# Windowed attention: the sink as a column of each head's scores, and sums transposed before they are inverted

## The chip, the cores and the metric

The kernel runs on one core of a Trainium2 chip. The metric is the device time of one execution in microseconds (us); lower is better. The core's engines run their own queues of instructions, in the order in which the program lists them: PE (matrix multiplies and transposes; PEld is its weight load), DVE (vector), ACT (scalar, here the exponentials and copies), POOL (general), SP (which issues most of the transfers). An instruction that waits for a semaphore holds everything behind it on its own engine.

## The reference

One layer of a diffusion transformer on 1024 latent tokens with 256 context tokens, width 1024: two attention parts side by side, merged by gates, then a SwiGLU feed-forward part with a convolution. The change lies in the first attention part: 8 heads in 2 groups of 4 that share keys and values, each block of 128 queries against its neighbouring blocks and the context, with one learned sink logit per head that takes part in the softmax but has no value.

```python
def _sink_softmax(scores, sink):
    sink = sink.astype(jnp.float32)[:, :, None, None]
    m = jnp.maximum(jnp.max(scores, axis=-1, keepdims=True), sink)
    e = jnp.exp(scores - m)
    return e / (jnp.sum(e, axis=-1, keepdims=True) + jnp.exp(sink - m))
...
        band = ((jnp.abs(q_pos[:, None] - k_pos[None, :]) <= WINDOW)
                & (k_pos[None, :] >= 0) & (k_pos[None, :] < n_tok))
        mask = jnp.concatenate([band, ctx_mask], axis=1)
        scores = jnp.where(mask, _gqa_scores(q_blk, k_blk), -jnp.inf)
        return _gqa_values(_sink_softmax(scores, sink), v_blk)
```

The second attention part is global: every query against all 1024 latent and 256 context keys, without a sink.

## The kernel before

Matrix operands are split into a high and a low part, so that most products are two or three multiplies. Attention fills the stretch from about 333 to 756 us of the span. It is made of 32 **units**: 16 of the windowed part (`br` 0), then 16 of the global part (`br` 1). A unit is one block `i` of 128 queries and one group `g` of four heads; names in the profile carry `br_i_g` and the head or key block behind it. In the windowed part a head has 256 latent columns for the first and last block, 384 for the others, and 256 context columns: 512 or 640 columns of scores.

What a unit does, with the lines of the profile:

- `lat(h)`, four times: PE multiplies queries and keys into the score tile `s` (two such tiles exist). DVE (L497) writes the negated scores to a tile `p` and keeps their running minimum with the negated sink, which gives `nm`, the negated maximum. ACT (L464) overwrites `p` with exp(score - maximum) and accumulates the row sum into `sm`. In the global part the context columns of all four heads are reduced beforehand (`cxp`, L515, tile `p_x`) and have an exponential and a sum `smc` of their own.
- `norm` (L518 to L525): in the windowed part DVE adds the sink to `nm` (L522, `f`), ACT takes the exponential of that (L523), DVE adds it to the sums (L524) and inverts the four columns of sums (L525). In the global part DVE adds `smc` to `sm` and inverts.
- `rows` (L527 to L538): PE transposes the 128x4 inverted sums to 4x128 (`str`, L529), ACT copies them into the tile `rb` (L532), and three transfers on SP's queue spread them over the partitions of `rb`, by way of DRAM. Two `rb` tiles exist.
- `value_steps`: for each key block PE transposes `p` of the four heads (`ptr`, L562), ACT makes the high part (`pth`, L571) and DVE the low part (`ptl`, L572), or POOL both for a few blocks; PE multiplies both with the values into `av` (L583, L584). At the end (`out_step`) ACT copies `av` out, POOL moves its upper half down, DVE adds the halves in the windowed part (`ot`, L595; in the global part POOL does), and POOL multiplies by `rb` and splits the result for the next product.

The value steps of a unit run among the scores of the next. The order on each engine is fixed when the program is built, by a scheduler that places the instructions by their data and buffers; the loop over `units` only gives it the steps. Tiles `p` come from a ring of eight in the pool `att`, used in turn by all units of both parts, so a new unit's first tiles lie on those of the unit two before it. Beside attention POOL and the transfers prepare weights for the next stage (`lwb`), which needs neither PE nor DVE here.

## Time and profile before

| | |
|---|---|
| median of 3 runs | 1546.9 us (1546.41 to 1548.97) |
| the profiled execution, its own time | 1549.18 us |
| its span, first to last instruction | 1547.4 us |
| granted clock of PE, mean | 0.998 |
| windowed units | from 336 to about 470 us of the span |
| global units | from about 462 to 756 us |
| one windowed unit in the steady part | 8.36 us (its sums' transpose at 399.44, the next unit's at 407.80) |

The profile counts times from the start of the span. A row of the timeline gives start, length, engine, line, operation and tiles of one instruction (or of several alike), and in brackets how long the engine had stood idle before it and whose result ended that. A row of the windows gives for a stretch the busy time and the instructions of PE, PEld, DVE, ACT and POOL, then the clock, the share of the transfer engines and GB/s. A row of a tile's view gives the shortest, the median and the longest length of its instructions in ns.

### The profile page before, as it was taken

How to read it: one execution, taken by the hardware profiler on the slowest of the kernel's cores; microseconds unless marked ns; L12 is line 12 of the kernel's file. 1: busy time of each engine (PE TensorE's matmuls, PEld its weight loads, DVE VectorE, ACT ScalarE, POOL GpSimd, SP SyncE). 2: the span in 40 equal slices, each digit the busy share in tenths (PEclk: the TensorE clock that was granted, in tenths of full speed). 3: DMA queues.
4: the chain of work that ended last, by engine and by line, in shares of the span. 5: the costliest groups of instructions: out<-in, count | busy, mean ns of one | idle time of the engine just before them, and what ended most of it. 6: DMA issues, size and time to landing. Idle time of an engine off the chain costs nothing.

```text
span 1547.4 us, 21962 instructions
## 1 busy us (share of the span) xinstructions
PE 1524.8 (99%) x7652; PEld 1269.2 (82%) x7652; DVE 1172.8 (76%) x1783; ACT 801.9 (52%) x1420; POOL 751.8 (49%) x697
## 2 busy tenths in 40 slices
PE   9999999999999999999999999999999999999997
PEld 7888888878887788888788988888888888888886
DVE  7588847638888667788575879898888887657797
ACT  5422223448888666698422674544444444435543
POOL 0375303426667466565423555766676675021063
PEclk9999999999999999999999999999999999999999
DMA  9667663322237565533452223233334446996723
GB/s 379 236 224 252 232 236 93 113 80 70 64 88 179 113 144 130 116 87 83 157 142 76 83 82 123 89 116 109 109 109 112 114 115 170 360 287 213 257 87 109
DMA packets 111873, 229.73 MB, mean 148 GB/s; under 512 B 13489, under 2 KB 27313, under 8 KB 111666
## 3 DMA queue, kind: packets, MB, share of 16 engines
q1 hardware_dynamic: 96464, 199.20, 38.5%
q0 software_dynamic: 10400, 20.19, 8.4%
q10 hardware_dynamic: 4898, 8.94, 1.6%
q8 instruction: 60, 0.98, 0.3%
q14 instruction: 51, 0.42, 0.1%
HBM read 177.09 MB, written 65.87 MB: 157 GB/s over the span
## 4 chain that ended last, share of the span: by engine, by line
PE 92%; DVE 4%; ACT 2%; issue 1%; POOL 1%; DMA 0%; DVEq 0%; ACTq 0%; POOLq 0%
PE ptr L562 6%; PE g L96 4%; PE g L95 4%; PE g L94 4%; PE p L94 4%; PE p L96 4%; PE p L95 4%; PE b L94 3%; PE b L96 3%; PE b L95 3%; PE av L583 3%; PE av L584 3%; PE s L451 3%; PE s L452 2%; PE c L95 2%; PE d L95 2%
## 5 line engine op out<-in xcount | busy, mean ns | idle before, releaser
L572 DVE TENSOR_TENSOR ptl<-ptr,pth 128x512 fp32r<-128x512 f32 x188 | 123.4, 684 | 32.6 <-ACT pth L571 31.8
L91 DVE TENSOR_TENSOR ld<-rd,hd 128x1024 fp32r<-128x1024 f32 x77 | 97.5, 1285 | 48.6 <-ACT hd L86 45.0
L562 PE MATMUL ptr<-ident,p 128*128 128x128 f32 x816 | 127.0, 277 | 5.8 <-DVE ptl L572 2.7
L571 ACT CAST pth<-ptr 128x512 fp32r<-128x512 f32 x188 | 105.6, 586 | 50.2 <-PE ptr L562 35.3
L464 ACT ACTIVATE p<-p,nm 128x1024 f32<-128x1024 f32 (+2 forms) x128 | 125.1, 979 | 10.5 <-DVE p L497 9.9
L86 ACT CAST hd<-rd 128x1024 fp32r<-128x1024 f32 x77 | 79.5, 1050 | 84.6 <-PE p L96 50.8
L562 PEld LDWEIGHTS ptr<-ident,p 128*128 128x128 f32 x816 | 95.1, 140 | 33.7 <-DVE ptl L572 7.7
L583 PE MATMUL av<-pth,VT 128*128 128x512 f32 x236 | 105.0, 445 | 1.2 <-ACT pth L571 0.9
L94 PE MATMUL p<-hd 128*128 128x512 f32 x264 | 103.2, 391 | 0.0
L96 PE MATMUL p<-hd,ld 128*128 128x512 f32 x264 | 102.7, 389 | 0.0
L95 PE MATMUL p<-ld,hd 128*128 128x512 f32 x264 | 102.7, 389 | 0.0
L96 PE MATMUL g<-hh,wlg 128*128 128x512 f32 x256 | 99.7, 390 | 0.4 <-POOL wlg L91 0.4
L94 PE MATMUL g<-hh,whg 128*128 128x512 f32 x256 | 99.9, 390 | 0.0
L95 PE MATMUL g<-hl,whg 128*128 128x512 f32 x256 | 99.6, 389 | 0.0
L584 PE MATMUL av<-ptl,VT 128*128 128x512 f32 x236 | 97.5, 413 | 0.5 <-POOL ptl L91 0.5
L91 POOL TENSOR_TENSOR wlg<-wg,whg 128x512 fp32r<-128x512 f32 x32 | 45.2, 1420 | 99.6 <-ACT whg L86 85.2
L497 DVE TENSOR_SCALAR_CACHE_REDUCE p<-s,cvt,nmc 128x1024 f32<-128x1024 f32 x64 | 84.5, 1338 | 7.4 <-PE ptr L562 5.5
L451 PE MATMUL s<-KL,q 128*128 128x512 f32 (+2 forms) x192 | 77.0, 401 | 0.8 <-DVE p_x L515 0.6
L88 POOL TENSOR_SCALAR pth<-prw 128x512 fp32r<-128x512 f32 x48 | 30.9, 644 | 93.1 <-PE av L583 43.8
L86 ACT CAST wS<-s 128x512 fp32r<-128x512 f32 x76 | 45.3, 621 | 52.0 <-POOL s L1166 51.2
L452 PE MATMUL s<-KL,q 128*128 128x512 f32 (+2 forms) x192 | 71.5, 372 | 0.0
L86 ACT CAST wA<-ru 128x512 fp32r<-128x512 f32 x57 | 35.5, 623 | 60.5 <-PE d L96 32.4
(403 smaller groups left out, 4922.5 us busy)
## 6 DMA issues: line engine op xcount, KB each, us to landing
wml<-in_wmodT_dram SPq DMA_DIRECT2D x48, 512.0 KB
ru<-in_w_up_dram SPq DMA_DIRECT2D x38, 512.0 KB
rd<-td SPq DMA_DIRECT2D x55, 256.0 KB
...
```

Source lines behind the costliest of these rows:

```text
L86: cast[:] = [nc.scalar.copy(hi, src).ins]
L91: low[:] = [lo_eng.tensor_tensor(out=lo, in0=src, in1=hi.bitcast(F32), op=ALU.subtract).ins]
L94: nc.tensor.matmul(ps, a[0], b[0], start=start, stop=False, skip_group_check=resumed)
L95: nc.tensor.matmul(ps, a[0], b[1], start=False, stop=False, skip_group_check=resumed)
L96: return nc.tensor.matmul(ps, a[1], b[0], start=False, stop=stop, skip_group_check=resumed).ins
L451: nc.tensor.matmul(o, self.q[0][:, hs], ks, start=True, stop=False)
L464: nc.scalar.activation(p, s, AF.Exp, bias=nm[:, h:h + 1], scale=scale, accum_out=sm[:, h:h + 1])
L562: nc.tensor.transpose(tr[:, h * P:(h + 1) * P], self.pslice(h, n), ident)
L571: nc.scalar.copy(hi, tr)
L572: nc.vector.tensor_tensor(out=lo, in0=tr, in1=hi.bitcast(F32), op=ALU.subtract)
L583: nc.tensor.matmul(self.av, v, hi, start=first, stop=False)
L584: nc.tensor.matmul(self.av, v, lo, start=False, stop=self.left == 0)
```

## The change

The sink becomes a column. Eight fixed tiles `pa0` to `pa7` of 128x1024 take the place of the ring in the windowed part, one for each head (`g*4+h`). At the start DVE copies each head's negated sink once into column 641 of its tile (L830, eight copies of 128x1). A head's negated scores now end at column 640, right before it, and start at column `pad`+1. The exponential reads scores and sink together and writes them one column further left, so the sink's column is read, never overwritten, and serves all eight units of that head; its exponential lands in column 640, is in the accumulated sum, and is not read by the transposes. The instructions of L522, L523 and L524 of the windowed part are gone.

Sums are transposed first. PE transposes `sm` itself, and the reciprocal, now 4x128 on DVE from the transposed tile into `rb` (L531), takes the place of ACT's copy, in all 32 units. The reciprocal 128x4 of L525 is gone; of `norm` only the addition of `smc` in the global part is left.

The tiles `p` move from `att` to a pool of their own, `pp`, on the other side of the memory. After unit 15 it is released and allocated again as a ring of eight for the global part. In the built program `pa0` to `pa7` lie in ascending places; in the new ring `p1_0_0_x` lies on `pa0`, and `p1_0_0_0` to `p1_0_0_3` lie on `pa7`, `pa6`, `pa5`, `pa4`, the tiles of unit 15 (`0_7_1`). Before, `p1_0_0_0` to `p1_0_0_2` lay on tiles of unit 14 and only `p1_0_0_3` on one of unit 15.

Line numbers of the changed kernel are a few higher or lower: L497 became L500, L464 L466, L515 L520, L529 L528, L562 L561, L571 and L572 L570 and L571, L583 and L584 L582 and L583, L595 L594, L1047 L1055.

```diff
@@ -47,6 +47,7 @@
 GORD = 3, 4, 4, 1, 4
 PWB = 5
 DAH = 3
+SINK = 640
 D3AT = (7, 5), (7, 9), (4, 1), (4, 4), (4, 7), (4, 10), (5, 2)
 NXS = 5
 RAWB = 3
@@ -455,13 +456,14 @@
             self.nm = small(f"nm_{self.id}", (P, 4))
             self.sm = small(f"sm_{self.id}", (P, 4))
             self.other = negsink[:, self.g * 4:self.g * 4 + 4]
+            self.pad = 0 if self.br else SINK - NC - self.w
 
         def qscale(self, t):
             return t[:, self.i, self.g * 4:self.g * 4 + 4]
 
-        def soft(self, s, p, h, nm, sm, scale):
+        def soft(self, s, p, h, sm):
             with tc.issue_after(first_exp):
-                nc.scalar.activation(p, s, AF.Exp, bias=nm[:, h:h + 1], scale=scale, accum_out=sm[:, h:h + 1])
+                nc.scalar.activation(p, s, AF.Exp, bias=self.nm[:, h:h + 1], scale=-1.0, accum_out=sm[:, h:h + 1])
 
         def lat(self, h):
             kh = self.br * 2 + self.g
@@ -493,13 +495,16 @@
                 self.qk(s[:, 512:512 + NC], h, KC[0][:, kh])
                 o = s[:, 512 - w:512 + NC]
             hs = slice(h, h + 1)
-            p = p_tile(f"p{self.id}_{h}")[:, 0:T if self.br else self.w + NC]
-            nc.vector.tensor_scalar(out=p, in0=o, scalar1=self.qscale(nqs)[:, hs] if self.br else -1.0,
+            p = p_tile(f"p{self.id}_{h}") if self.br else pa[self.g * 4 + h]
+            sc = p if self.br else p[:, self.pad + 1:SINK + 1]
+            nc.vector.tensor_scalar(out=sc, in0=o, scalar1=self.qscale(nqs)[:, hs] if self.br else -1.0,
                                     scalar2=self.other[:, hs], op0=ALU.mult, op1=ALU.min, accum_out=self.nm[:, hs])
-            self.soft(p, p, h, self.nm, self.sm, -1.0)
-            self.pc[h, 0] = p
             if self.br:
-                self.soft(self.pc[h, 1], self.pc[h, 1], h, self.nm, self.smc, -1.0)
+                self.soft(p, p, h, self.sm)
+                self.soft(self.pc[h, 1], self.pc[h, 1], h, self.smc)
+            else:
+                self.soft(p[:, self.pad + 1:SINK + 2], p[:, self.pad:SINK + 1], h, self.sm)
+            self.pc[h, 0] = p[:, self.pad:]
 
         def cxp(self):
             kh = self.br * 2 + self.g
@@ -516,20 +521,14 @@
                                         op0=ALU.mult, op1=ALU.min, accum_out=self.other[:, h:h + 1])
 
         def norm(self):
-            hc = slice(self.g * 4, self.g * 4 + 4)
-            more = self.smc if self.br else small(f"f_{self.id}", (P, 4))
-            if not self.br:
-                nc.vector.tensor_tensor(out=more, in0=self.nm, in1=sinkb[:, hc], op=ALU.add)
-                nc.scalar.activation(more, more, AF.Exp)
-            nc.vector.tensor_tensor(out=self.sm, in0=self.sm, in1=more, op=ALU.add)
-            nc.vector.reciprocal(self.sm, self.sm)
+            nc.vector.tensor_tensor(out=self.sm, in0=self.sm, in1=self.smc, op=ALU.add)
 
         def rows(self):
             tr = pt_tile(f"str{self.id}")
             nc.tensor.transpose(tr[0:4, 0:P], self.sm, ident)
             self.rb = att.tile([P, 2, P], F32, tag="rb", name=f"rb{self.id}", bufs=2)
             row = self.rb[0:4, 0]
-            nc.scalar.copy(row, tr[0:4, 0:P])
+            nc.vector.reciprocal(row, tr[0:4, 0:P])
             dn = dpool.tile([4, P], F32, tag=f"dn{self.id}", name=f"dn{self.id}")
             tokens.append(f"dn{self.id}")
             nc.sync.dma_start(dn, row)
@@ -539,7 +538,7 @@
 
         def score_steps(self):
             steps = [lambda h=h: self.lat(h) for h in range(4)]
-            return steps + [self.norm]
+            return steps + [self.norm] * self.br
 
         def context(self):
             self.begin()
@@ -825,8 +824,13 @@
     def s_tile(name):
         return ps2.tile([P, T], F32, tag="s", name=name, bufs=2)
 
+    pp = tc.alloc_tile_pool(name="pp", bufs=1, side="right", reuse_waits="tile")
+    pa = [pp.tile([P, T], F32, tag=f"pa{n}", name=f"pa{n}") for n in range(8)]
+    for n in range(8):
+        nc.vector.tensor_copy(pa[n][:, SINK + 1:SINK + 2], negsink[:, n:n + 1])
+
     def p_tile(name):
-        return att.tile([P, T], F32, tag="p", name=name, bufs=8)
+        return pp.tile([P, T], F32, tag="p", name=name, bufs=8)
 
     def small(name, shape):
         return att.tile(list(shape), F32, tag=name.split("_")[0], name=name,
@@ -898,6 +902,9 @@
             ss = units[u].score_steps()
             if u + 2 < nu:
                 ss.append(units[u + 2].qprep)
+        if u == 16:
+            pp.release()
+            pp = tc.alloc_tile_pool(name="pp", bufs=1, side="right", reuse_waits="tile")
         if u == 29:
             first = branch_steps(1, w_b, (0, 1), att, (nc.gpsimd, nc.gpsimd), (0,),
                                  lambda: [ht(f"{a}wb1_0", (P, 8, P), R32) for a in "hl"])
@@ -932,6 +939,7 @@
     hput(*[f"VT{t}" for t in range(5)])
     first[2]()
     ps2.release()
+    pp.release()
     att.release()
     qp.release()
 
```

Three places show how the order moved, all on DVE. The first is the **start of the windowed part**, where `lnx` is the last instruction before attention, `s0_0_0_h` are the scores of the first unit and `s0_0_1_h` those of the second. Before:

```order
L1047 TENSOR_TENSOR lnx_68<-ln1c_66,modc_60 128x8 [waits Activation_49]
L497 TENSOR_SCALAR p0_0_0_0_3038,nm_0_0_0_3030<-s0_0_0_0_3032,negsink_63 128x512 [waits PE_49]
L497 TENSOR_SCALAR p0_0_0_1_3047,nm_0_0_0_3030<-s0_0_0_1_3041,negsink_63 128x512 [waits PE_49,Pool_49]
L497 TENSOR_SCALAR p0_0_0_2_3056,nm_0_0_0_3030<-s0_0_0_2_3050,negsink_63 128x512 [waits PE_49]
L497 TENSOR_SCALAR p0_0_0_3_3065,nm_0_0_0_3030<-s0_0_0_3_3059,negsink_63 128x512 [waits DMAHW3_49,DMAHW1_49,DMAHW7_49,DMAHW0_49,PE_49]
L497 TENSOR_SCALAR p0_0_1_0_3103,nm_0_0_1_3086<-s0_0_1_0_3097,negsink_63 128x512 [waits DMAHW2_49,PE_49]
L522 TENSOR_TENSOR f_0_0_0_3068<-nm_0_0_0_3030,sinkb_64 128x4 [waits DVE_49]
L497 TENSOR_SCALAR p0_0_1_1_3112,nm_0_0_1_3086<-s0_0_1_1_3106,negsink_63 128x512 [waits PE_49]
L524 TENSOR_TENSOR sm_0_0_0_3031<-sm_0_0_0_3031,f_0_0_0_3068 128x4 [waits Activation_49]
L525 RECIPROCAL sm_0_0_0_3031<-sm_0_0_0_3031 128x4 [waits DVE_49]
```

And with the change:

```order
L1055 TENSOR_TENSOR lnx_68<-ln1c_66,modc_60 128x8 [waits Activation_49]
L830 COPY pa0_3033<-negsink_63 128x1 [waits PE_49]
L830 COPY pa1_3034<-negsink_63 128x1
L830 COPY pa2_3035<-negsink_63 128x1
L830 COPY pa3_3036<-negsink_63 128x1
L830 COPY pa4_3037<-negsink_63 128x1 [waits DMAHW3_49,DMAHW2_49,DMAHW7_49,DMAHW1_49,Pool_49]
L830 COPY pa5_3038<-negsink_63 128x1 [waits DMAHW3_49,DMAHW0_49]
L830 COPY pa6_3039<-negsink_63 128x1 [waits PE_49]
L830 COPY pa7_3040<-negsink_63 128x1 [waits PE_49]
L500 TENSOR_SCALAR pa0_3033,nm_0_0_0_3049<-s0_0_0_0_3051,negsink_63 128x512 [waits PE_49]
L500 TENSOR_SCALAR pa1_3034,nm_0_0_0_3049<-s0_0_0_1_3059,negsink_63 128x512 [waits PE_49]
L500 TENSOR_SCALAR pa2_3035,nm_0_0_0_3049<-s0_0_0_2_3067,negsink_63 128x512 [waits PE_49]
```

Eight copies stand between `lnx` and the first score reduction; the first, fifth and sixth of them, with those of `pa6` and `pa7`, carry the waits for the memory that the tiles take over. The sink's three small instructions of the first unit no longer stand among the second unit's reductions.

The second is a **unit of the steady part**, the norm of unit `0_4_0` among the scores of `0_4_1`, with the values of `0_3_1` before it. Before:

```order
L595 TENSOR_TENSOR ot0_3_0_4059<-avs0_3_0_4055,up0_3_0_4057 64x256 [waits Pool_49]
L595 TENSOR_TENSOR ot0_3_0_4059<-avs0_3_0_4055,up0_3_0_4057 64x256
L522 TENSOR_TENSOR f_0_4_0_4065<-nm_0_4_0_3976,sinkb_64 128x4 [waits DVE_49]
L524 TENSOR_TENSOR sm_0_4_0_3977<-sm_0_4_0_3977,f_0_4_0_4065 128x4 [waits Activation_49]
L525 RECIPROCAL sm_0_4_0_3977<-sm_0_4_0_3977 128x4 [waits DVE_49]
L497 TENSOR_SCALAR p0_4_1_0_4127,nm_0_4_1_4108<-s0_4_1_0_4121,negsink_63 128x640 [waits PE_49]
L572 TENSOR_TENSOR ptl0_3_1_4_4103<-ptr0_3_1_4_4097,pth0_3_1_4_4102 128x512 [waits Activation_49]
L572 TENSOR_TENSOR ptl0_4_0_0_4116<-ptr0_4_0_0_4110,pth0_4_0_0_4115 128x512 [waits Activation_49]
L572 TENSOR_TENSOR ptl0_4_0_1_4136<-ptr0_4_0_1_4130,pth0_4_0_1_4135 128x512 [waits Activation_49]
L497 TENSOR_SCALAR p0_4_1_1_4145,nm_0_4_1_4108<-s0_4_1_1_4139,negsink_63 128x640 [waits PE_49]
```

And with the change:

```order
L571 TENSOR_TENSOR ptl0_3_1_4_4041<-ptr0_3_1_4_4035,pth0_3_1_4_4040 128x512 [waits DVE_49,Activation_49]
L500 TENSOR_SCALAR pa4_3037,nm_0_4_1_4046<-s0_4_1_0_4059,negsink_63 128x640 [waits PE_49]
L500 TENSOR_SCALAR pa5_3038,nm_0_4_1_4046<-s0_4_1_1_4076,negsink_63 128x640 [waits PE_49]
L571 TENSOR_TENSOR ptl0_4_0_0_4054<-ptr0_4_0_0_4048,pth0_4_0_0_4053 128x512 [waits DVE_49,Activation_49]
L571 TENSOR_TENSOR ptl0_4_0_1_4073<-ptr0_4_0_1_4067,pth0_4_0_1_4072 128x512 [waits DVE_49,Activation_49]
L531 RECIPROCAL rb0_4_0_4086<-str0_4_0_4084 4x128 [waits DMAHW1_49,DMAHW0_49,DMAHW5_49,PE_49,Pool_49]
L500 TENSOR_SCALAR pa6_3039,nm_0_4_1_4046<-s0_4_1_2_4092,negsink_63 128x640 [waits PE_49]
L571 TENSOR_TENSOR ptl0_4_0_2_4106<-ptr0_4_0_2_4100,pth0_4_0_2_4105 128x512 [waits Activation_49]
```

Where `f`, `sm` and the 128x4 reciprocal stood ahead of the next unit's first reduction, one 4x128 reciprocal stands two reductions later; it waits for PE's transpose, for transfers and for POOL.

The third is the **hand-over** from the last windowed unit (15, `0_7_1`) to the first global one (16, `1_0_0`). Before:

```order
L515 TENSOR_SCALAR p1_0_0_x_5038,nmc_1_0_0_5036<-s1_0_0_x_5027,cvt_69 128x256 [waits PE_49]
L515 TENSOR_SCALAR p1_0_0_x_5038,nmc_1_0_0_5036<-s1_0_0_x_5027,cvt_69 128x256
L524 TENSOR_TENSOR sm_0_7_1_4905<-sm_0_7_1_4905,f_0_7_1_4970 128x4 [waits Activation_49]
L515 TENSOR_SCALAR p1_0_0_x_5038,nmc_1_0_0_5036<-s1_0_0_x_5027,cvt_69 128x256
L525 RECIPROCAL sm_0_7_1_4905<-sm_0_7_1_4905 128x4 [waits DVE_49]
L595 TENSOR_TENSOR ot0_6_1_4992<-avs0_6_1_4988,up0_6_1_4990 64x256 [waits Pool_49]
L595 TENSOR_TENSOR ot0_6_1_4992<-avs0_6_1_4988,up0_6_1_4990 64x256
L515 TENSOR_SCALAR p1_0_0_x_5038,nmc_1_0_0_5036<-s1_0_0_x_5027,cvt_69 128x256
L572 TENSOR_TENSOR ptl0_7_1_0_5049<-ptr0_7_1_0_5043,pth0_7_1_0_5048 128x512 [waits PE_49,Activation_49]
L497 TENSOR_SCALAR p1_0_0_0_5059,nm_1_0_0_5025<-s1_0_0_0_5054,cvt_69,nmc_1_0_0_5036 128x1024 [waits PE_49]
L497 TENSOR_SCALAR p1_0_0_1_5068,nm_1_0_0_5025<-s1_0_0_1_5063,cvt_69,nmc_1_0_0_5036 128x1024 [waits PE_49]
L572 TENSOR_TENSOR ptl0_7_1_1_5078<-ptr0_7_1_1_5072,pth0_7_1_1_5077 128x512 [waits Activation_49]
```

And with the change:

```order
L571 TENSOR_TENSOR ptl0_7_1_0_4928<-ptr0_7_1_0_4922,pth0_7_1_0_4927 128x512 [waits Activation_49]
L531 RECIPROCAL rb0_7_1_4973<-str0_7_1_4971 4x128 [waits DMAHW2_49,DMAHW1_49,DMAHW5_49,PE_49,Pool_49]
L571 TENSOR_TENSOR ptl0_7_1_1_4957<-ptr0_7_1_1_4951,pth0_7_1_1_4956 128x512 [waits DVE_49,Activation_49]
L571 TENSOR_TENSOR ptl0_7_1_2_4995<-ptr0_7_1_2_4989,pth0_7_1_2_4994 128x512 [waits Activation_49]
L520 TENSOR_SCALAR p1_0_0_x_4917,nmc_1_0_0_4915<-s1_0_0_x_4906,cvt_69 128x256 x4
L500 TENSOR_SCALAR p1_0_0_0_4938,nm_1_0_0_4904<-s1_0_0_0_4933,cvt_69,nmc_1_0_0_4915 128x1024 [waits DVE_49,PE_49]
L500 TENSOR_SCALAR p1_0_0_1_4947,nm_1_0_0_4904<-s1_0_0_1_4942,cvt_69,nmc_1_0_0_4915 128x1024 [waits DVE_49,PE_49]
L500 TENSOR_SCALAR p1_0_0_2_4967,nm_1_0_0_4904<-s1_0_0_2_4962,cvt_69,nmc_1_0_0_4915 128x1024 [waits DVE_49,PE_49]
L500 TENSOR_SCALAR p1_0_0_3_4984,nm_1_0_0_4904<-s1_0_0_3_4979,cvt_69,nmc_1_0_0_4915 128x1024 [waits DVE_49,PE_49]
```

The four context reductions of unit 16 (`p1_0_0_x`) stood ahead of unit 15's first low part; they now stand behind its first three low parts and its reciprocal. Unit 16's four score reductions carry a wait for PE and DVE each.

## Prediction

> **What bounds the kernel now.** First the page: the span, the busy shares and the chain of waits.
>
> ```profile
> span 1547.4 us, 21962 instructions
> PE 1524.8 (99%) x7652; PEld 1269.2 (82%) x7652; DVE 1172.8 (76%) x1783; ACT 801.9 (52%) x1420; POOL 751.8 (49%) x697
> PE 92%; DVE 4%; ACT 2%; issue 1%; POOL 1%; DMA 0%; DVEq 0%; ACTq 0%; POOLq 0%
> ```
>
> PE is busy 99% of the span and holds 92% of the chain that ended last. The change takes no work from PE: the same transposes and products are left, among them one transpose of sums per unit. So time can only come from, or go into, the few places where PE waits, and a cheaper softmax elsewhere is worth nothing by itself. The windows show how unequal the stretches are (busy us of PE, PEld, DVE, ACT, POOL).
>
> ```profile
> 400.00:420.00 20.00, 19.95 (x134) 17.00 (x134) 17.82 (x41) 16.89 (x40) 12.43 (x20) 1.00 0.24 70
> 470.00:480.00 10.00, 8.77 (x47) 6.36 (x46) 8.57 (x21) 9.98 (x24) 6.15 (x9) 1.00 1.03 248
> 500.00:600.00 100.00, 98.38 (x559) 81.69 (x558) 67.37 (x138) 63.91 (x137) 53.55 (x64) 1.00 0.54 120
> ```
>
> In the steady windowed stretch PE idles 0.05 of 20 us, with DVE at 89% right behind it. In the hand-over to the global part it idles 1.23 of 10. In the global part DVE is busy 67%. The clock is 1.00 throughout, so no difference is to be expected from it. The timeline of PE names the gaps worth looking at (start, length, and in brackets the idle time before).
>
> ```profile
> 337.72 0.33 PE L562 MATMUL ptr<-ident,p 128*128 128x128 f32 x1 [1.39 <-ACT p L464]
> 346.36 0.66 PE L562 MATMUL ptr<-ident,p 128*128 128x128 f32 x4 [1.47 <-DVE ptl L572]
> 474.40 0.33 PE L562 MATMUL ptr<-ident,p 128*128 128x128 f32 x1 [0.71 <-ACT p L464]
> ```
>
> Two lie at the start of the windowed part, one in the hand-over. These, and the near-tie of PE and DVE between them, are where the change can act.
>
> **What it removes and what it adds.** The tile's view gives the prices (shortest, median, longest in ns).
>
> ```profile
> L525 DVE RECIPROCAL sm<-sm x32: 160/177/179, 340.8 to 739.9; 128x4 f32<-128x4 f32 x32
> L524 DVE TENSOR_TENSOR sm<-sm,f x16: 156/479/592, 340.6 to 463.6; 128x4 f32<-128x4 f32 x16
> L522 DVE TENSOR_TENSOR f<-nm,sinkb x16: 150/163/2275, 339.4 to 462.3; 128x4 f32<-128x4 f32 x16
> L532 ACT COPY rb<-str x32: 238/255/257, 342.9 to 743.0; 4x128 f32<-4x128 f32 x32
> ```
>
> Per windowed unit DVE loses 163 + 479 + 177 = 0.82 us, and a wait for ACT between `f` and `sm`; ACT loses the exponential of `f` and a copy of 255 ns, and gains one column of 641 in each exponential, which is nothing. DVE gains the 4x128 reciprocal in all 32 units. No row has that operation, so its price R is the unknown of this case.
>
> Lower bound of R: a single pass over 128 columns. Two score reductions below, 0.75 us at 512 columns and 0.85 to 0.88 at 640, give about 1.0 ns per column, so 177 ns + 124 columns x 1.0 ns = 0.30 us. Upper bound: at four columns the reciprocal takes 14 ns longer than the addition of L522 (177 against 163). If all of that is repeated division, it falls on the three columns after the first: 14 / 3 + 1.0 = 5.7 ns per column, and 177 + 124 x 5.7 = 0.88 us; with 9 ns, allowing for an addition that is itself dearer than a plain one-operand instruction, 1.2 us. I take **R = 0.9**, since the four-column row is the only one with the operation in it. The Trainium skill, "VectorE: DVE Perf Modes", section "First, the fixed hardware budget", says that the reciprocal divides iteratively with a repeat count of 8; read as eight passes per column that would be an estimate of about 1.2 us, and the sum below would come to +1.5 instead of +0.3. The row lies between one pass and eight, and nearer to eight.
>
> **The start.** The timeline of DVE, with POOL's `lwb`:
>
> ```profile
> 335.97 0.17 DVE L1047 TENSOR_TENSOR lnx<-ln1c,modc 128x8 f32<-128x8 f32 x1 [28.64 <-ACT lnx L804]
> 336.06 0.75 DVE L497 TENSOR_SCALAR_CACHE_REDUCE p<-s,negsink 128x512 f32<-128x512 f32 x1
> 339.41 0.17 DVE L522 TENSOR_TENSOR f<-nm,sinkb 128x4 f32<-128x4 f32 x1
> 339.62 0.75 DVE L497 TENSOR_SCALAR_CACHE_REDUCE p<-s,negsink 128x512 f32<-128x512 f32 x1
> 340.62 0.16 DVE L524 TENSOR_TENSOR sm<-sm,f 128x4 f32<-128x4 f32 x1 [0.24 <-ACT f L523]
> 340.91 0.72 DVE L497 TENSOR_SCALAR_CACHE_REDUCE p<-s,negsink 128x512 f32<-128x512 f32 x1
> 343.32 2.37 POOL L91 TENSOR_TENSOR lwb<-rwb,hwb 128x1024 fp32r<-128x1024 f32 x1
> 343.43 2.27 DVE L522 TENSOR_TENSOR f<-nm,sinkb 128x4 f32<-128x4 f32 x1
> 345.63 0.68 DVE L572 TENSOR_TENSOR ptl<-ptr,pth 128x512 fp32r<-128x512 f32 x1
> 347.03 0.59 DVE L524 TENSOR_TENSOR sm<-sm,f 128x4 f32<-128x4 f32 x1
> 347.75 0.85 DVE L497 TENSOR_SCALAR_CACHE_REDUCE p<-s,negsink 128x640 f32<-128x640 f32 x1
> ```
>
> DVE works without a pause here, PE waits for it, and so DVE's clock is the stage's clock. The second unit's `f` stood 2.27 us, from just after POOL began `lwb` until POOL was done; PE's gap of 1.47 follows from it. Taken out, by the starts of the rows: 339.41 to 339.62 (0.21), the norm of the first unit with its wait (340.38, where the reduction of 339.62 leaves off after its 0.75, to 340.91: 0.53), 343.43 to 345.63 (2.20), and 347.03 to 347.75 (0.72). Together 3.66 us. Put in: two reciprocals, 2 x 0.9 = 1.80; about 0.35 in which they stand waiting for PE's transpose of the sums, which DVE did not wait for before; and the eight copies ahead of the first reduction. `lnx` to the first reduction is a step of 0.09, so 8 x 0.09 = 0.72. Gain: 3.66 - 1.80 - 0.35 - 0.72 = **0.8 us**. With R = 0.3 it is 2.0, with R = 1.2 it is 0.2. If POOL holds the copies as it held `f`, up to the 2.2 us of that one is gone again; I don't count it, since it met one `f` of 16 (their median is 163 ns). The gain's ends are 2.0 and -2.0.
>
> **The steady windowed units**, around the norm of one:
>
> ```profile
> 399.44 0.27 PE L529 MATMUL str<-ident,sm 128*4 128x128 f32 x1
> 403.32 0.94 DVE L595 TENSOR_TENSOR ot<-avs,up 64x256 f32<-64x256 f32 x2
> 404.28 0.16 DVE L522 TENSOR_TENSOR f<-nm,sinkb 128x4 f32<-128x4 f32 x1
> 405.46 0.48 DVE L524 TENSOR_TENSOR sm<-sm,f 128x4 f32<-128x4 f32 x1 [1.01 <-ACT f L523]
> 406.07 0.85 DVE L497 TENSOR_SCALAR_CACHE_REDUCE p<-s,negsink 128x640 f32<-128x640 f32 x1
> 406.85 1.88 DVE L572 TENSOR_TENSOR ptl<-ptr,pth 128x512 fp32r<-128x512 f32 x3
> 407.80 0.27 PE L529 MATMUL str<-ident,sm 128*4 128x128 f32 x1
> ```
>
> From transpose to transpose PE takes 8.36 us. DVE has four reductions at steps of 0.80, four low parts at 0.60 and 0.95 for `ot`, 6.55 us, to which the norm with its wait added 406.07 - 404.28 = 1.8: 8.35, as long as PE. With the change the 1.8 give way to R: 6.55 + 0.9 = 7.45, and about 0.6 of waiting behind the reciprocal, which stands in DVE's queue ahead of the next two reductions and low parts and waits for PE's transpose, for the transfers out of `rb` and for POOL's product two units earlier. 8.05 stays under 8.36, so PE hides it and the saving too: **0**. At R = 1.2 it is 8.35, a tie.
>
> **The hand-over.** Timeline from PE's transposes of unit 17's queries to the second value product of unit 16:
>
> ```profile
> 460.42 0.54 PE L441 MATMUL qtr<-identr,qs 128*128 128x128 f32 x4
> 464.48 0.85 DVE L595 TENSOR_TENSOR ot<-avs,up 64x256 f32<-64x256 f32 x2 [0.23 <-POOL up L591]
> 466.38 1.33 DVE L497 TENSOR_SCALAR_CACHE_REDUCE p<-s,cvt,nmc 128x1024 f32<-128x1024 f32 x1
> 467.63 1.34 DVE L497 TENSOR_SCALAR_CACHE_REDUCE p<-s,cvt,nmc 128x1024 f32<-128x1024 f32 x1
> 472.64 0.47 DVE L515 TENSOR_SCALAR_CACHE_REDUCE p_x<-s_x,cvt 128x256 f32<-128x256 f32 x1
> 473.04 0.48 DVE L515 TENSOR_SCALAR_CACHE_REDUCE p_x<-s_x,cvt 128x256 f32<-128x256 f32 x1
> 483.20 0.48 PE L583 MATMUL av<-pth,VT 128*128 128x512 f32 x1
> ```
>
> Before, 22.8 us lie between the first row and the last, and unit 16's first score reduction (466.38) ran among the transposes of unit 15, since its tile lay on one of unit 14. With the change it lies on a tile of unit 15, and DVE has the reciprocal and two more low parts of unit 15 ahead of the context reductions. In DVE's new order, from the same start: the transposed sums of unit 15 at 5.7 (PE's row of products by their steps); R to 6.6; two low parts to 7.8; four context reductions at 0.40 to 9.4; four score reductions at 1.26, with 0.75 + 0.1 + 0.2 of waiting for scores whose tiles the context reductions free late, to 15.5; `ot` 0.85 to 16.35; four context reductions of unit 17 to 17.95, a score reduction to 19.2; the sums' addition and two low parts to 20.6; a score reduction to 21.8; R to 22.7; a low part to 23.3; PE's transposes and a product to 23.9. So 23.9 against 22.8, **1.1 us** lost. R counts twice: nothing is lost at 0.3, 1.8 at 1.2.
>
> **The global part.** DVE trades a 177 ns reciprocal for R: 16 x 0.7 = 11.5 us more over some 290 us at 67% busy, with PE at 98%: covered, 0 (between -0.5 and +1.5, should the later `rb` or a held reciprocal meet one of PE's few gaps). The tiles of `rb` come later by R less ACT's 255 ns, and nothing waits for them but POOL's product.
>
> **The sum**: -0.8 + 0 + 1.1 + 0 = +0.3 us on the span of 1547.4. The profiled execution took 1549.18, 2.3 more than the median of 1546.9, so I put the difference on the median: **1547.2 us**. With both ends of R alone it runs from 1544.9 to 1548.5.
>
> **Rivals.** I count as no change what lies within 0.2%, 3.1 us, about what a measurement of this kernel can tell: 1543.8 to 1550.0.
>
> *Faster, the reciprocal is one pass.* R = 0.3: the start gains 2.0, the hand-over loses nothing, and DVE, now at 6.9 + 0.6 of 8.36, brings the low parts earlier, so that the small gaps of the following windowed units close too: 350 to 380 has PE idle 0.73 + 1.03 us by its windows.
>
> ```profile
> 350.00:360.00 10.00, 9.27 (x66) 8.27 (x65) 8.97 (x21) 8.01 (x20) 6.50 (x10) 1.00 0.22 55
> 360.00:380.00 20.00, 18.97 (x123) 15.61 (x122) 16.74 (x38) 16.49 (x40) 12.73 (x19) 1.00 0.26 74
> ```
>
> -2.0 - 1.7 = -3.7: 1543.2. For it: the four-column row differs by only 14 ns. Against it: one pass would make the rows of reciprocal and addition alike, and median and lower price both differ by 10 to 14 ns on four columns.
>
> *Slower, DVE becomes the bound of the windowed part.* It decides from R = 1.2 on, or when the wait for the transposed sums is longer than 0.6: then DVE needs more than 8.36 per unit. Each 0.3 over costs that in some 13 steady units, 13 x 0.3 = 3.9, and with the start and hand-over at R = 1.2 (+1.6) the sum is +5.5: 1552.4. For it: before, DVE was as full as PE, and the new wait is on the slower of two partners, PE, where ACT's answer came in 1.01. Against it: ACT's wait goes.
>
> *Slower, the hand-over drains.* All four score reductions of unit 16 stand behind the last transposes of unit 15, and PE has nothing but them to do: if ACT's exponentials (it is busy 9.98 of 10 at 470 to 480) start as late as the reductions, PE idles some 3 us more than the walk has: +3.3, 1550.2. Against it: the walk already has the reductions late.
>
> **Chances.** Forecast 0.36 (of that 0.04 faster, 0.22 no change, 0.10 slower, as its terms all lean on R); one pass 0.20 (0.16 faster, 0.04 same); DVE the bound 0.30 (0.28 slower, 0.02 same); drain 0.14 (0.11 slower, 0.03 same). Faster 0.20, same 0.31, slower 0.49. Range: down to 1543.2, the one-pass case, and up to 1552.5, where DVE is the bound; beyond these some 0.1 on each side. The forecast's own is 1544.9 to 1549.5.
>
> **What would show it.** A row of the 4x128 reciprocal near 0.9 us; PE's gap of 1.39 at 337 longer by some 0.7, the one of 1.47 gone; PE at 99.7% between 400 and 450 with DVE near 90%; the distance from unit 17's query transposes to unit 16's second value product near 23.9. The forecast is wrong if the windowed units' step rises over 8.36, if copies or reciprocals are held far beyond their price, or if the time moves in a stage after 756 us, which the change doesn't touch.

## The result, and the profile after

The changed kernel takes 1551.98 us (median of 8 runs, 1550.96 to 1552.96) against 1547.55 for the kernel before on the same chip: ratio 1.0028, 95% interval 1.0017 to 1.0039. It is slower by 4.4 us. The forecast was 1547.2, in a range of 1543.2 to 1552.5.

First the page of the changed kernel: span, engines, chain of waits.

```profile
span 1550.7 us, 21958 instructions
PE 1525.7 (98%) x7652; PEld 1269.7 (82%) x7652; DVE 1180.4 (76%) x1759; ACT 795.9 (51%) x1372; POOL 752.3 (49%) x697
PE 88%; DVE 6%; POOL 2%; issue 2%; DMA 1%; ACT 1%; SPq 0%; DVEq 0%; POOLq 0%; ACTq 0%
```

PE's work is the same to 0.9 us, and its share of the chain falls from 92 to 88%, while DVE's rises from 4 to 6. To see where, the span is cut at landmarks that both kernels have: the first score product, PE's transposes of the sums of units 4, 12 and 16 (rows `str` of the timeline), and the first product of the next stage, `y`. Each figure is the difference of the starts of two such rows.

| stretch, us | before | after | difference | forecast |
|---|---|---|---|---|
| to the first score | 333.53 | 333.69 | +0.16 | 0 |
| start: first score to sums of unit 4 | 40.84 | 39.89 | -0.95 | -0.8 |
| eight steady windowed units, to unit 12 | 66.87 | 69.09 | +2.22 | 0 |
| hand-over, to unit 16 | 39.12 | 40.62 | +1.50 | +1.1 |
| global part and end, to the first `y` | 314.32 | 314.90 | +0.58 | 0 |
| the rest | 752.73 | 752.47 | -0.26 | 0 |

The sum is +3.25 of the two profiled spans' 3.3. It is 1.1 less than the 4.4 between the medians, because the profiled execution of the kernel before took 1549.18, 1.6 over its median, and that of the change 1552.44, 0.5 over. The loss has one place that was not foreseen, the steady windowed units: 8.64 us each instead of 8.36. The windows of 366 to 456 us show it, before and then after (PE, PEld, DVE, ACT, POOL).

```profile
366.00:456.00 90.00, 89.37 (x594) 75.71 (x594) 77.63 (x185) 76.95 (x183) 57.82 (x87) 1.00 0.25 70
```

```profile
366.00:456.00 90.00, 87.29 (x583) 73.85 (x582) 84.37 (x159) 73.53 (x157) 59.72 (x85) 1.00 0.26 65
```

DVE has fewer instructions and more busy time, 94% against 86, and PE stands 2.7 us instead of 0.6. The tile's view of the changed kernel gives the new prices, the reciprocal's and that of `ot`:

```profile
L531 DVE RECIPROCAL rb<-str x32: 934/940/946, 343.4 to 747.4; 4x128 f32<-4x128 f32 x32
L594 DVE TENSOR_TENSOR ot<-avs,up x32: 403/737/1429, 354.9 to 487.0; 64x256 f32<-64x256 f32 x32
```

and the same view of the kernel before:

```profile
L595 DVE TENSOR_TENSOR ot<-avs,up x32: 415/419/1432, 355.2 to 483.0; 64x256 f32<-64x256 f32 x32
```

The reciprocal takes 0.94 us, where 0.9 was taken. But `ot`, two instructions per unit, went from a median of 0.42 each to 0.74. One steady unit of the changed kernel shows why, in the timelines of DVE and POOL:

```profile
399.69 0.88 DVE L500 TENSOR_SCALAR_CACHE_REDUCE pa<-s,negsink 128x640 f32<-128x640 f32 x1 [0.44 <-PE s L453]
401.75 0.94 DVE L531 RECIPROCAL rb<-str 4x128 f32<-4x128 f32 x1
403.93 1.63 DVE L594 TENSOR_TENSOR ot<-avs,up 64x256 f32<-64x256 f32 x2
405.59 0.89 DVE L500 TENSOR_SCALAR_CACHE_REDUCE pa<-s,negsink 128x640 f32<-128x640 f32 x1
403.75 0.78 POOL L92 TENSOR_TENSOR qs<-Q,qs 128x256 fp32r<-128x256 f32 x1
404.50 0.79 POOL L89 TENSOR_SCALAR pth<-prw 128x512 fp32r<-128x512 f32 x1
```

`ot` now runs from 403.93 to 405.56, beside POOL's `qs` and `pth`. Both sides are stretched: `ot` from 0.94 in the kernel before to 1.63, `pth` from 0.62 alone to 0.79. And the chain of waits of the changed kernel, from one unit's exponential to the next's, no longer runs along PE:

```profile
406.52 0.93 ACT pa L466 x2
407.45 0.04 issue
407.50 0.44 PE ptr L561 x2
407.94 0.12 PE s L489
408.06 0.12 PE s L452
408.17 0.13 PE s L453
...
409.22 0.62 DVE ptl L571 x2
...
410.38 0.94 DVE rb L531
...
412.03 0.60 DVE ptl L571
412.63 0.81 DVE ot L594
413.44 0.01 issue
413.45 0.74 DVE ot L594
414.19 0.03 issue
414.22 0.91 DVE pa L500 x2
415.13 0.02 issue
415.15 0.93 ACT pa L466 x2
```

415.15 - 406.52 = 8.63, the step of the unit. It is a closed loop: ACT's exponential, two transposes that wait for it, the scores behind them on PE, then DVE's whole row from the reduction of those scores (408.33) through low parts, reciprocal and `ot` to the reduction (414.22) on which the next exponential waits. DVE holds 6.8 us of it, with the reciprocal 0.94 and `ot` 1.55.

### The profile page after: what moved, and what is told of

Its sections match the earlier page's. It is cut to its first block, busy times and chain, and to the rows that moved or that the text cites. A ratio compares the mean times of both kernels' runs of the same rounds, so it can differ in the third digit from the quotient of the medians.

```text
span 1550.7 us, 21958 instructions
## 1 busy us (share of the span) xinstructions
PE 1525.7 (98%) x7652; PEld 1269.7 (82%) x7652; DVE 1180.4 (76%) x1759; ACT 795.9 (51%) x1372; POOL 752.3 (49%) x697
## 4 chain that ended last, share of the span: by engine, by line
PE 88%; DVE 6%; POOL 2%; issue 2%; DMA 1%; ACT 1%; SPq 0%; DVEq 0%; POOLq 0%; ACTq 0%
PE ptr L561 5%; PE g L97 4%; PE g L96 4%; PE g L95 4%; PE p L97 4%; PE p L96 4%; PE p L95 4%; PE b L95 3%; PE b L97 3%; PE b L96 3%; PE av L582 2%; PE av L583 2%; PE d L95 2%; PE c L97 2%; PE c L95 2%; PE d L97 2%
## 5 line engine op out<-in xcount | busy, mean ns | idle before, releaser
L571 DVE TENSOR_TENSOR ptl<-ptr,pth 128x512 fp32r<-128x512 f32 x188 | 124.1, 684 | 30.0 <-ACT pth L570 29.5
L570 ACT CAST pth<-ptr 128x512 fp32r<-128x512 f32 x188 | 106.1, 583 | 51.9 <-PE ptr L561 37.4
L582 PE MATMUL av<-pth,VT 128*128 128x512 f32 x236 | 105.1, 445 | 2.8 <-POOL pth L89 1.6
L583 PE MATMUL av<-ptl,VT 128*128 128x512 f32 x236 | 98.8, 419 | 2.1 <-POOL ptl L92 2.1
L500 DVE TENSOR_SCALAR_CACHE_REDUCE p<-s,cvt,nmc 128x1024 f32<-128x1024 f32 x64 | 84.7, 1339 | 7.8 <-PE ptr L561 4.9
L466 ACT ACTIVATE p<-p,nm 128x1024 f32<-128x1024 f32 x64 | 73.7, 1152 | 15.3 <-DVE p L500 14.6
L561 PE MATMUL ptr<-ident,p 128*128 128x128 f32 x512 | 75.3, 276 | 1.6 <-DVE ptl L571 0.7
L561 PEld LDWEIGHTS ptr<-ident,p 128*128 128x128 f32 x512 | 61.5, 141 | 17.1 <-DVE ptl L571 3.3
```

Of the source, the lines that this page charges most:

```text
L500: nc.vector.tensor_scalar(out=sc, in0=o, scalar1=self.qscale(nqs)[:, hs] if self.br else -1.0, scalar2=self.other[:, hs], op0=ALU.mult, op ...
L561: nc.tensor.transpose(tr[:, h * P:(h + 1) * P], self.pslice(h, n), ident)
L570: nc.scalar.copy(hi, tr)
L571: nc.vector.tensor_tensor(out=lo, in0=tr, in1=hi.bitcast(F32), op=ALU.subtract)
L582: nc.tensor.matmul(self.av, v, hi, start=first, stop=False)
L583: nc.tensor.matmul(self.av, v, lo, start=False, stop=self.left == 0)
```

## The experiments

All ratios are to the kernel before, run beside each on the same chip (medians of 1547.4 to 1547.8), with their 95% intervals. The stretches are those of the table above, each from one profiled execution.

| kernel | time, us | ratio | start | steady step | hand-over | global and end |
|---|---|---|---|---|---|---|
| before | 1547.55 | 1 | 40.84 | 8.36 | 39.12 | 314.3 |
| the change | 1551.98 | 1.0028 (1.0017 to 1.0039) | 39.89 | 8.64 | 40.62 | 314.9 |
| e1_invert_first | 1545.81 | 0.9986 (0.9977 to 0.9995) | 40.73 | 8.05 | 41.80 | 312.0 |
| e2_two_reciprocals | 1560.58 | 1.0079 (1.0066 to 1.0093) | 41.73 | 8.99 | 42.74 | 314.3 |
| e3_ot_on_pool | 1565.37 | 1.0113 (1.0098 to 1.0128) | 39.27 | 9.33 | 48.48 | 312.9 |
| e4_tiles_reversed | 1553.41 | 1.0034 (1.0021 to 1.0046) | 40.31 | 8.64 | 42.21 | 315.0 |
| e5_no_release | 1576.45 | 1.0182 (1.0166 to 1.0197) | 40.18 | 8.64 | 40.73 | 339.5 |
| e6_first_no_release | 1565.12 | 1.0107 (1.0092 to 1.0122) | 40.83 | 8.04 | 46.40 | 325.9 |
| e7_late_without_column | 1549.63 | 1.0014 (1.0004 to 1.0023) | 39.79 | 8.43 | 40.87 | 314.5 |
| e8_short_reciprocal | 1552.89 | 1.0032 (1.0021 to 1.0043) | 39.99 | 8.76 | 41.09 | 314.4 |
| e9_late_in_global_only | 1548.16 | 1.0004 (0.9995 to 1.0013) | 40.83 | 8.04 | 41.81 | 314.8 |
| e10_copy_for_reciprocal | 1547.83 | 1.0002 (0.9993 to 1.0011) | 38.66 | 8.38 | 40.40 | 314.8 |
| e11_column_in_ring | 1544.84 | 0.9983 (0.9975 to 0.9992) | 39.23 | 8.02 | 40.69 | 312.7 |
| e12_no_pool_at_end | 1546.56 | 0.9996 (0.9987 to 1.0005) | 39.77 | 8.04 | 40.86 | 313.6 |

**The clock in single traces.** In some of these traces the granted clock of PE falls for a few us, each time behind a pause of PE of 1.2 us or more, but not behind each such pause. By windows of 5 us, each times what its clock lacks to 1.00, PE loses 1.7 us at each place (3.4 in e5's global part). The places in the table's stretches (runs named by their numbers) are the start of e1, e3, e4, e5, e6, e8 and e9 (335 to 345 us), the hand-over of e2 (475 to 485), e3 (450 and 480), e4 (470) and e6 (480), and the global part of the change, e4, e5, e9 and e10 (610 to 635). It does not come with the kernel alone: by their edits e1 and e12 differ only from unit 14 on, and at the start e1 is seen with a clock of 0.83 in 335 to 345 and takes 40.73 us, e12 with 1.00 and takes 39.77. Differences of 1 to 2 us between two stretches count only where both have such a place or neither has. The steady units have no such place in any of the traces.

**Which of the two parts costs.** The change does two things, so each was made alone. First the column without the late inversion:

```diff
         def norm(self):
-            nc.vector.tensor_tensor(out=self.sm, in0=self.sm, in1=self.smc, op=ALU.add)
+            if self.br:
+                nc.vector.tensor_tensor(out=self.sm, in0=self.sm, in1=self.smc, op=ALU.add)
+            nc.vector.reciprocal(self.sm, self.sm)
...
-            nc.vector.reciprocal(row, tr[0:4, 0:P])
+            nc.scalar.copy(row, tr[0:4, 0:P])
...
-            return steps + [self.norm] * self.br
+            return steps + [self.norm]
```

> The sink's column and the fixed tiles stay; the sums are inverted as 128x4 on DVE ahead of the transpose again, and ACT copies the transposed rows, in all 32 units. Theory L (a loop through DVE sets the windowed units' step: DVE's reduction, ACT's exponential, PE's transposes and scores, and DVE's row of work with the 0.94 us reciprocal and a slowed ot in it): DVE loses about 0.8 us per unit, the steady step goes from 8.63 back to PE's 8.36, and the time falls by 3 us or more against the change, to before -1 to -3 (ratio 0.998 to 0.9995). Rival C (the column or the fixed tiles hold up the units): the step stays at 8.5 or more and the time within 1 us of the change.

The steady step fell to 8.05, below the 8.36 of the kernel before, and the whole is 6.2 us under the change and 0.14% faster than before. The column is a gain; the rival falls. The step went further down than expected, since 8.36 was taken for PE's own pace. DVE's timeline now has room: from one pair of low parts to the next, 396.05 to 404.11, two waits of 1.09 and 0.30 leave it idle:

```profile
396.05 1.29 DVE L573 TENSOR_TENSOR ptl<-ptr,pth 128x512 fp32r<-128x512 f32 x2 [0.30 <-ACT pth L572]
401.66 0.88 DVE L596 TENSOR_TENSOR ot<-avs,up 64x256 f32<-64x256 f32 x2
403.63 0.18 DVE L526 RECIPROCAL sm<-sm 128x4 f32<-128x4 f32 x1 [1.09 <-ACT pa L466]
404.11 1.29 DVE L573 TENSOR_TENSOR ptl<-ptr,pth 128x512 fp32r<-128x512 f32 x2 [0.30 <-ACT pth L572]
```

Then the late inversion without the column, an edit of the kernel before:

```diff
             nc.vector.tensor_tensor(out=self.sm, in0=self.sm, in1=more, op=ALU.add)
-            nc.vector.reciprocal(self.sm, self.sm)
...
-            nc.scalar.copy(row, tr[0:4, 0:P])
+            nc.vector.reciprocal(row, tr[0:4, 0:P])
```

> The kernel before with one part of the change alone: sums transposed first, then inverted as 4x128 on DVE, in all 32 units; the sink stays an exponential and an addition of its own, and the ring of tiles stays. Theory L: the 0.87 comes into DVE's row, which was full at 8.36 with its wait for ACT, and 0.09 goes; the steady step is 8.9 to 9.15 and the time 6 to 10 us over before. Rival: late inversion costs only beside the column (by the order that comes of both); the step stays below 8.5.

It costs 0.07 per steady unit, not 0.5 to 0.8: theory L's sum of DVE's row falls here, and its rival holds. In the timeline of DVE the wait that stood between `f` and the sums is in part filled with a low part (0.39 of it is left), and `ot` keeps its short time:

```profile
400.85 0.94 DVE L531 RECIPROCAL rb<-str 4x128 f32<-4x128 f32 x1
403.04 0.84 DVE L594 TENSOR_TENSOR ot<-avs,up 64x256 f32<-64x256 f32 x2
403.90 0.46 DVE L522 TENSOR_TENSOR f<-nm,sinkb 128x4 f32<-128x4 f32 x1
404.75 0.69 DVE L571 TENSOR_TENSOR ptl<-ptr,pth 128x512 fp32r<-128x512 f32 x1 [0.39 <-ACT pth L570]
405.36 0.39 DVE L524 TENSOR_TENSOR sm<-sm,f 128x4 f32<-128x4 f32 x1
```

So the four steps are 8.36 (neither), 8.05 (column), 8.43 (late inversion) and 8.64 (both). Late inversion costs 0.07 without the column and 0.59 with it: the two parts do not add. The program's order is made anew each time, and only with both is `ot` stretched to 1.63 beside POOL's work (0.88 with the column alone, 0.84 with late inversion alone); that this is the reason is argued from the rows, not tried by itself.

**Is it the reciprocal's length, or its place?** Three runs changed the length, and one took `ot` off DVE.

```diff
             nc.vector.reciprocal(row, tr[0:4, 0:P])
+            if not self.br:
+                nc.vector.reciprocal(row, tr[0:4, 0:P])
```

> The change with the 4x128 reciprocal issued twice in each windowed unit (the second writes the same rows again). Theory L: DVE's row sets the step, so each steady unit grows by the reciprocal's 0.87, to about 9.5 us, and the time by 11 to 14 us against the change (about 1564). Rival W (not DVE's work but its waiting for PE's transposed sums or for rb's transfers sets the step): the second reciprocal falls into idle time, the step rises by less than 0.4 and the time by less than 6.

The step rose by 0.35, which W allows; L's 0.87 falls as it was put. The 0.44 that DVE had waited is gone from its row, and 8.64 + 0.87 - 0.44 = 9.07 is near the 8.99 measured; but the chain of waits of this kernel runs by ACT and PE, not DVE. The time rose by 8.6 us, and of that 1.7 is the clock in the hand-over and 1.9 lies behind the first `y`, which the edit doesn't touch, so the time does not decide between the two.

```diff
-            nc.vector.reciprocal(row, tr[0:4, 0:P])
+            if self.br:
+                nc.vector.reciprocal(row, tr[0:4, 0:P])
+            else:
+                nc.scalar.copy(row[:, 16:P], tr[0:4, 16:P])
+                nc.vector.reciprocal(row[:, 0:16], tr[0:4, 0:16])
```

> The change with the late reciprocal over 16 of the 128 columns in the windowed part, and a copy on ACT for the other 112, whose sums are so left uninverted. By 0.94 us at 128 columns and 0.18 at 4 it takes 0.25 us. Theory L (its length in DVE's row is what costs): the steady step falls from 8.63 to 8.1 or less. Rival W (its place, where DVE waits for PE's transposed sums and for rb): the step stays above 8.4.

The 4x16 reciprocal took 0.24 us, as expected, and yet the steps alternate between 8.06 and 9.45. The chain of waits of this kernel runs through POOL in the long ones:

```profile
397.55 0.74 POOL O L92
398.29 0.59 POOL pth L89
398.88 0.07 issue
398.95 1.28 POOL ptl L92
400.24 0.04 issue
400.28 0.50 PE av L587
```

Its new order left POOL's pooled low part late. L is not refuted by this (every second unit is at 8.06), but neither is it shown.

```diff
-            nc.vector.reciprocal(row, tr[0:4, 0:P])
+            (nc.vector.reciprocal if self.br else nc.vector.tensor_copy)(row, tr[0:4, 0:P])
```

> The change with a copy on DVE in place of the late reciprocal in the windowed part, whose values are so multiplied by the sums instead of their inverses; the inversion is left out. By the score reductions' 1.0 ns per column the copy takes 0.3 us instead of 0.94; the program's order moves at some places with it. Theory L (the reciprocal's length, with the ot slowed beside POOL, fills DVE's part of a loop): the steady step falls to 8.2 or less. Rival O (the order that comes with a transpose ahead of DVE's row decides, as e8_short_reciprocal hints): 8.4 or more.

The copy took 0.27. The mean step is 8.38, between the two expectations; six of eight are 7.95 to 8.15, and every fourth is 9.37, again behind POOL. Against the change it is 4.2 us faster: 0.67 us less in DVE's row, with the order that comes of it, is worth 0.26 per unit on the mean and 1.2 at the start. So shortening it pays; how much of that is its length and how much the order is open, since no run here changed the one and kept the other.

```diff
-                e = nc.gpsimd if self.br else nc.vector
+                e = nc.gpsimd
```

> The change with the addition ot of the windowed part on POOL instead of DVE. Theory L: 1.63 us leave DVE's row per unit, the step falls to PE's 8.36, and the time by 2 to 3 us against the change (about 1549.5). Rival P: POOL, 66% busy there and 1.5 us per unit more, comes late with the rows and the pooled low parts, and the step stays at 8.6 or more.

POOL is no place for `ot`: the steps are 8.6 to 10.3, and the hand-over takes 48, of which up to 3.4 is the clock at its two places. The rival holds; the loop's need for `ot` could not be tried so.

**The hand-over.** Here the forecast named the tiles' places: unit 16's first tiles lie on unit 15's.

```diff
-    pa = [pp.tile([P, T], F32, tag=f"pa{n}", name=f"pa{n}") for n in range(8)]
+    pa = [pp.tile([P, T], F32, tag=f"pa{n}", name=f"pa{n}") for n in range(7, -1, -1)][::-1]
```

> The change with the eight fixed tiles allocated in reverse order, so that unit 16's first score tiles lie on those of unit 14 instead of unit 15. Theory T (the overlap of tiles makes the hand-over longer): from the transposed sums of 442.67 to those of 483.30 the 40.6 us fall to 39.6 or less, and the time by 1 to 1.5 us against the change. Rival: the order of DVE's work, with the reciprocals in it, sets the hand-over and the 40.6 stay within 0.3. The steady step stays at 8.63 by both.

The row of the table is longer by 1.6, but the trace has PE's clock at 0.66 there. The windows of 470 to 475 us, the change first, then this run:

```profile
470.00:475.00 5.00, 3.79 (x19) 2.94 (x17) 4.32 (x12) 2.81 (x6) 4.54 (x6) 1.00 0.81 240
```

```profile
470.00:475.00 5.00, 4.10 (x11) 3.24 (x12) 3.25 (x11) 2.58 (x6) 3.92 (x6) 0.66 0.91 260
```

In both kernels PE comes out of a pause of 1.21 behind ACT's `avs`. From the product behind it to the next transposes of `p` the same 20 products take 4.71 us in the change and 6.27 here, eight of their steps at 0.43 instead of 0.23. These 1.56 are the whole difference: without them the hand-over is 40.65 against 40.62, within the 0.3 of the rival, and theory T shows no gain. The edit is no clean test of it, for reversed, the context tile `p1_0_0_x`, which comes first, falls on `pa7`, a tile of unit 15; in the timeline of DVE its reduction waits for the transposes:

```profile
469.73 0.48 DVE L520 TENSOR_SCALAR_CACHE_REDUCE p_x<-s_x,cvt 128x256 f32<-128x256 f32 x1 [0.22 <-PE ptr L561]
```

The next two took away the release, with the global part using the fixed tiles in turn:

```diff
     def p_tile(name):
-        return pp.tile([P, T], F32, tag="p", name=name, bufs=8)
+        turn[0] += 1
+        return pa[(turn[0] - 1) % 8]
...
-        if u == 16:
-            pp.release()
-            pp = tc.alloc_tile_pool(name="pp", bufs=1, side="right", reuse_waits="tile")
```

> The change without the release between the parts: the global part takes the eight fixed tiles in turn (pa0 for the first context tile, pa1 and on for the scores). DVE's order has unit 16's context reductions and first score reductions among unit 15's low parts again, as before. Theory B (the released pool is a barrier: no tile of the new ring is written before all transposes of unit 15, wherever the tiles lie): from the transposed sums of unit 12 to those of unit 16 the 40.6 us fall to 39.1 or less, as before, and the time by 1.5 us or more against the change. Rival: the reciprocals in the row of unit 15 and 16 set it, and it stays above 40.2. The steady step stays at 8.63.

> The same without the release, with the sums inverted ahead of the transpose as in e1_invert_first. Theory B: the 41.8 us from unit 12 to unit 16 of that kernel fall to about 39, with the steady step at 8.06, and the time by 2 to 3 us against it, to 0.9965 to 0.9975 of before. Rival: POOL and ACT, which held PE there too, keep it above 41, and the time is that of e1_invert_first.

From unit 17 on a tile is taken in turn while an earlier unit's probabilities in it are still to be read, so values of the global part are computed from overwritten tiles, and these two say nothing on that part. Up to unit 16 they are as meant: 40.73 and 46.40, not shorter (the 46.40 have a pause of PE of 3.07 behind POOL's `ptl` in them, and the clock behind it). Theory B falls in both.

```diff
-            p = p_tile(f"p{self.id}_{h}") if self.br else pa[self.g * 4 + h]
+            p = p_tile(f"p{self.id}_{h}")
+            if not self.br:
+                nc.vector.tensor_copy(p[:, SINK + 1:SINK + 2], self.other[:, hs])
...
-        return pp.tile([P, T], F32, tag="p", name=name, bufs=8)
+        return att.tile([P, T], F32, tag="p", name=name, bufs=8)
```

(with the pool `pp` and its eight copies gone, and the edit of e1_invert_first).

> The sink's column with the ring of tiles of the kernel before: no fixed tiles and no released pool, the column copied into each head's tile by DVE (128x1, 64 times, steps of 0.06), sums inverted ahead of the transpose. Theory R (fixed tiles and their release cost in the hand-over): from unit 12's to unit 16's transposed sums 39 to 40 us, against 41.8 of e1_invert_first, with a steady step of 8.06 to 8.2 for DVE has room; time 1 to 2.5 us under e1_invert_first. Rival (POOL and ACT limit the hand-over, and what the windowed part gains is lost there in waiting): 41 us or more and no gain.

The hand-over is 40.69, 1.1 shorter than that of e1_invert_first and between the two expectations; the start is 1.5 shorter too, but some 1.0 of that is the clock in e1's trace (e12 has 39.77 without it). Its time, 1544.84, is the best of all, though its interval overlaps that of e1_invert_first.

```diff
-                pooled = n in POOL_LO[self.br]
+                pooled = n in POOL_LO[self.br] and (self.br or self.i < NT - 1)
```

> e1_invert_first with the pooled low part of units 14 and 15 on ACT and DVE instead of POOL. Rival of the above (POOL limits the hand-over): PE's gaps there that end on POOL's low parts, 1.03 and 1.15, go, and the hand-over falls from 41.8 to 40.5 or less. Theory R: it stays above 41.

40.86: 0.9 off with the tiles and the release kept, so POOL has a share nearly as large as the ring's. The gap of 1.15 is gone, the one of 1.03 stays (1.02, at 455), behind a low part of an earlier unit that the edit leaves on POOL. No gain in all: 1546.56. What makes before's 39.12 shorter than every other kernel's hand-over is not settled by these runs.

**The global part.**

```diff
+            if not self.br:
+                nc.vector.reciprocal(self.sm, self.sm)
...
+            (nc.vector.reciprocal if self.br else nc.scalar.copy)(row, tr[0:4, 0:P])
```

> The windowed part as in e1_invert_first (column, inverted first), the global part as in the change (transposed first). Theory G (in the global part the late inversion costs nothing by itself, but with it POOL's order has the weight split hwb1_0, which waits for its load, ahead of a pooled block of unit 22 or 23): the steady windowed step is 8.06, PE's two gaps near 613 us, 1.57 and 0.85 in the change, are there again, and the time is 1 to 3 us over e1_invert_first (1547 to 1549). Rival: that gap comes of the windowed part's being late, and the time is that of e1_invert_first.

2.35 us over e1_invert_first, with the same windowed part to 0.1 us, and both gaps are there (1.56 and 0.85): that is theory G, and its rival falls. In the changed kernel, timelines of POOL and PE:

```profile
607.01 2.39 POOL L92 TENSOR_TENSOR lwb<-rwb,hwb 128x1024 fp32r<-128x1024 f32 x1
613.04 1.04 POOL L89 TENSOR_SCALAR hwb<-rwb 128x1024 fp32r<-128x1024 f32 x1 [3.64 <-DMA rwb<-in_w_b_dram]
614.05 0.62 POOL L89 TENSOR_SCALAR pth<-prw 128x512 fp32r<-128x512 f32 x1
614.72 0.50 PE L582 MATMUL av<-pth,VT 128*128 128x512 f32 x1 [1.57 <-POOL pth L89]
616.08 0.50 PE L583 MATMUL av<-ptl,VT 128*128 128x512 f32 x1 [0.85 <-POOL ptl L92]
```

POOL stands 3.64 us on a load of weights that the next stage needs, with the pooled block that PE needs queued behind it. In the kernel before, e1, e11 and e12, which invert first in the global part, `pth` stands ahead of that split, and the two gaps aren't there.

The price of it is less than the 2.35. In the traces of e9 and e1 the stretch differs by 2.73: unit 22 to 23 takes 21.70 against 17.43, and unit 18 to 19 takes 20.23 against 21.89, where two gaps of e1 near 530 us (0.87 and 0.60) are not in e9. And the clock of e9 is 0.77 and 0.89 in the windows from 610 to 620; in e2, e3, e7 and e8, which have the same two gaps at a clock of 1.00, unit 22 to 23 takes 20.13 to 20.32. So about 1.5 of the 2.73 is the clock and 1.2 the late inversion. Without the column, e7 against the kernel before, it is 0.2.

## Why the prediction was right or wrong

**The range and the likeliest time.** The range held the time; the likeliest time was 4.8 us low, and the case that came true in kind was the second rival, DVE as the bound of the windowed part (given 0.30, and 1552.4). That its time lies 0.4 from the measured one is luck: it put 3.9 on the steady units and 1.6 on start and hand-over, and the traces show 2.2 and 0.55. By the prediction's own sign, a step over 8.36, the case that it forecast is wrong.

**R** was right: 0.9 taken, 0.94 measured. By 0.18 us at 4 columns, 0.24 at 16 and 0.94 at 128 it costs 6.2 ns per column, some six of the score reductions' 1.0 ns. The Trainium skill, "VectorE: DVE Perf Modes", section "First, the fixed hardware budget", has a repeat count of 8; read as eight passes per column that was an estimate of 1.2 us, and these rows say six. No run shows the 9 ns per column behind the upper bound of 1.2.

**The start** was right in size, -0.8 forecast and -0.95 measured, with some luck in its terms. The eight copies took a step of 0.49, not 0.72, and were not held by POOL; the second unit's `f` and PE's gap of 1.47 are gone. But the reciprocals did not wait 0.35 for the transposed sums; DVE waited for scores instead, 0.41, 0.17 and 1.20 between 340 and 348. The first gap grew by 0.54, and smaller gaps of 0.81 and 0.39 came behind it. Timelines of DVE and PE:

```profile
336.22 0.57 DVE L830 COPY pa<-negsink 128x1 f32<-128x1 f32 x8
336.71 0.74 DVE L500 TENSOR_SCALAR_CACHE_REDUCE pa<-s,negsink 128x512 f32<-128x512 f32 x1
338.42 0.33 PE L561 MATMUL ptr<-ident,pa 128*128 128x128 f32 x1 [1.93 <-ACT pa L466]
349.28 0.50 PE L583 MATMUL av<-ptl,VT 128*128 128x512 f32 x1 [0.81 <-POOL ptl L92]
```

**The steady units** are the step that failed: "8.05 stays under 8.36, so PE hides it and the saving too: 0". Two of its premises were wrong. The walk kept `ot` at 0.95, a price from the old order; in the new order it stands beside POOL's work and takes 1.63. With it the walk gives 6.55 + 0.70 + 0.87 + 0.44 = 8.56 of the 8.64 measured. And 8.36 was not PE's floor: with the column alone the same products take 8.05, so the saving was not hidden either. The rival named R or the wait for the transposed sums as the point from which it decides; it was neither: R is 0.94, and DVE's wait in the unit, 0.44, is for scores. How much of the lost 0.28 comes of the reciprocal's length and how much of the new order stays open.

**The hand-over** had about the right size, +1.1 against +1.5; by the walk's own landmarks, unit 17's query transposes to unit 16's second block of values, it is 23.55 against 22.78, +0.8. The walk along DVE's row came true, each point 0.3 earlier or so: from unit 17's query transposes the context reductions end at 9.14 (9.4 forecast), the four score reductions at 15.17 (15.5), `ot` at 16.04 (16.35). The reason given for the new order, the score tile's lying on one of unit 15, is not shown: with the tiles reversed the stretch is the same but for the clock, and then it is the context tile that lies on one of unit 15. Beside early inversion the ring instead of fixed tiles is worth 1.1 and POOL's blocks 0.9, and neither explains before's 39.12.

**The global part** came to +0.58, inside the bounds of -0.5 and +1.5, but only by luck. The prediction expected no difference from the clock, and in the trace of the change it is 0.73 and 0.93 in the windows from 615 to 625: unit 22 to 23 takes 21.81, some 1.5 more than the 20.13 to 20.32 at full clock, so that about -1 would be left by this estimate. Nor does nothing else move: late inversion costs about 1.2 beside the column and 0.2 without it in these traces, with the two gaps through POOL's order, while the kernels with the column that invert first are 0.7 to 2.3 under before in this stretch. Why they are is not settled; 1.3 of e1's 2.3 lies behind unit 31, where before has a gap of 0.88 (at 756.17) and e1 none.

**The first rival**, a reciprocal of one pass, is refuted by its row. **The drain** did not come in its form: PE's gaps in the hand-over are 1.21 behind ACT's `avs` and five of 0.27 to 0.45, some 1.6 us more than before, not 3.
